# Own slots for the first gate, and an earlier place for the last tile's gates, in the recurrent branch of a two-layer streaming encoder

## The chip, the cores and the metric

The kernel runs on one core of one Trainium2 chip. The metric is the device time of one execution in microseconds (us), as the median of three runs. Profiles and traces come from one further execution that was taken with the hardware profiler; times inside it are counted from the start of its span.

Of the engines, PE is TensorE (matmuls into PSUM), ACT is ScalarE (activations, casts), DVE is VectorE, POOL is GpSimd, and SP issues nearly all DMAs. Each of them works through its own instructions in a fixed order and waits on semaphores of the others.

## What is computed

The reference is two layers over 1152 tokens (1024 of a prompt, 8 samples of 16). The change lies in layer 0, in the recurrent branch of its mixer, so only that is shown. `xr` and `gr` are two 512-wide column groups of one input projection.

```python
def causal_conv(xr, buf, w, b):
    t = xr.shape[1]
    xp = jnp.concatenate([buf.astype(xr.dtype), xr], axis=1)
    y = xp[:, 0:t] * w[0] + b
    for i in range(1, CONV_W):
        y = y + xp[:, i:i + t] * w[i]
    return y, xp[:, -(CONV_W - 1):]

def rg_lru(xc, h0, wa, ba, wx, bx, lam):
    ...
    r = jax.nn.sigmoid(jnp.einsum('btnc,ncd->btnd', xb, wa).reshape(bsz, t, D_LRU) + ba)
    gi = jax.nn.sigmoid(jnp.einsum('btnc,ncd->btnd', xb, wx).reshape(bsz, t, D_LRU) + bx)
    log_a = -LRU_C * r.astype(jnp.float32) * jax.nn.softplus(-lam.astype(jnp.float32))
    a = jnp.exp(log_a)
    bterm = jnp.sqrt(-jnp.expm1(2.0 * log_a)) * (gi * xc).astype(jnp.float32)
    bterm = bterm.at[:, 0].add(a[:, 0] * h0.astype(jnp.float32))
    ...
    _, h = lax.associative_scan(combine, (a, bterm), axis=1)

    # in even_mixer
    xc, new_buf = causal_conv(xr, conv_buf, conv_w, conv_b)
    hs, new_h = rg_lru(xc, h0, wa, ba, wx, bx, lam)
    rec = hs * jax.nn.gelu(gr)
    out = jnp.concatenate([att, rec], axis=-1) @ w_out
```

The rest of layer 0 is sliding-window attention, the output projection and an MLP; layer 1 is a gated MLP with a spatial mixing and a second MLP.

## The kernel before, in words

Everything is kept feature-major: 128 features lie on the partitions and the tokens run along the free dimension. The recurrent branch has 512 features, so four feature tiles, c = 0 to 3. The tokens are cut into three blocks of 384 (`NB`). A float32 matmul is done as three passes (`three`, L531 to L533) over a high and a low part of both operands; one bank of a projection is 8 slices of the contraction times 3 passes, so 24 matmuls.

For each feature tile there are three kinds of steps, and `LRU_ORDER` (L267) sets the order in which the program writes them:

- `x` with a number is one block of the first branch (`xr_bank`): 24 matmuls, and DVE scales the bank into `pad` (L679, L681). After the third block the convolution is queued in the background list: one ACT pass (L575), three DVE passes into `y` (L578), and the split of the result into `xch` (ACT, L586) and `xcl` (DVE, L590).
- `G` is `gates(c)`: two gates of three column pieces each, so six PSUM banks (`ax`) of 3 matmuls, 18 matmuls for a tile, each bank read by an ACT sigmoid (L613) into a tile `rg` of the gate. The first gate, `rg0`, is r and becomes a; the second, `rg1`, is gi and becomes the input of the recurrence. `gates` then queues in the background the rest of the recurrence: gi times y on POOL (L633), tanh, exp and sqrt on ACT (L624, L627, L630), two products on DVE (L636, L639), the samples' start states (L644 to L646), the scan on DVE (L649), which writes the state tile `h`, and two small copies of `h` on POOL (L653, L654).
- `g` is one block of the second branch (`gr_bank`): 24 matmuls, DVE scales the bank into `u` (L696), and after the third block ACT applies a gelu (L700) and POOL multiplies `h` by it (L703, L705).

`pump` hands out background work and splits of weights (`W.split`, L200 and L201: an ACT cast into the high part, a DVE subtraction into the low part) between the banks. The Tile framework then schedules all of it: each engine gets one fixed list of instructions that may differ from the written order. From the attention's first instruction on the recorded order is kept by the helper at L257.

The buffers matter here. `lr("rg", ...)` (the pool `lru`, two buffers to a tag) has two slots for all eight gate tiles: `rg0` and `rg1` of a tile take both, so the next tile's sigmoids can't write before this tile's scan has read them. The tag `xb` has four slots of 128 partitions and some 1176 floats: the four input tiles xin0 to xin3 at first, and later the four states `h`. The tag `y` has two slots for the convolution results. There are five `ax` banks, so PE can compute five of a tile's six gate banks ahead of the sigmoids. `raw` has two slots for loaded weights, and 12 split halves (`w`, `wx`) are alive at most in this stage, so the last two halves of the attention's q weights (w28 and w29) take slots that the last `g` bank frees.

After the last `g` block comes the attention. Its first token tile needs 24 matmuls for q and 24 for k and v (L257, `mm` from `w` and `xn0h`, `xn0l`, `xn1h`, `xn1l`; eight steps of three q and three kv matmuls), ACT copies both banks into `raw`, POOL squares it into `rstd`, DVE and POOL do the norm and the rotation, and PE transposes the result (`tp` from `xa`). PE does the second token tile's 48 matmuls before that first transpose.

Of the kernel before, what the change touches and what calls it, by code (L numbers as in the profile page):

```python
# [10 lines left out]
F32 = mybir.dt.float32  # L11
# [8 lines left out]
P = 128  # L20
# [12 lines left out]
CW = PADW - 3  # L33
# [230 lines left out]
         "n25 s06 s07 m11 f0 n27 m01 s10 n21 s11 s12 n23 s13 n20 s14 s15 s20 s16 n26 n22 F0 s21 n24 m02 e00 m12 s22 s23 "  # L264
         "s17 e10 s24 s25 f1 s26 s27 F1 e01 e11 f2 F2 e02 e12")

LRU_ORDER = [(t[0], int(t[1])) for t in "x2 x2 x2 x3 G0 g0 x3 G1 g0 x3 G2 g0 g1 g1 g1 g2 g2 g2 G3 g3 g3 g3".split()]  # L267

NKT, NVV, NPB = 3, 3, 3
QEV = False  # L270
# [11 lines left out]
def body(ctx, tc, io):  # L282
    nc = tc.nc

    def pool(name, bufs=1, space=None):
        kw = {} if space is None else {"space": space}
        return ctx.enter_context(tc.tile_pool(name=name, bufs=bufs, **kw))
# [4 lines left out]
    xp = pool("x")  # L292
# [31 lines left out]
    def bank(tag):  # L324
        bank.n += 1
        p = banks[tag if tag in ("mm", "two") else "ax"].pool
        return p.tile([P, 1024 if tag == "two" else 512], F32, tag=tag, bufs=BANKS[tag], name=f"{tag}{bank.n}")
# [47 lines left out]
    order += [(("xr", 0), [xr[0]], None), (("xr", 1), [xr[1]], None)]  # L375
    for kind, c in LRU_ORDER:
        key = {"x": ("xr", c), "G": ("gate", c // 2), "g": ("gr", c)}[kind]
# [21 lines left out]
    def pump(act, dve, pl, halves=1):  # L399
        W.pump(halves)  # L400
        bg.pump(act, dve, pl)
# [13 lines left out]
    def lr(tag, name, shape=None, dt=F32):  # L415
        return lrp.tile(shape or [P, CW], dt, tag=tag, bufs=2, name=name)
# [113 lines left out]
    def three(ps, wh, wl, ah, al, start, stop):  # L530
        nc.tensor.matmul(ps, wh, ah, start=start, stop=False)  # L531
        nc.tensor.matmul(ps, wh, al, start=False, stop=False)  # L532
        nc.tensor.matmul(ps, wl, ah, start=False, stop=stop)  # L533
# [38 lines left out]
    def add_conv(c):  # L572
        def c0():
            conv[c] = lr("y", f"y{c}")
            nc.scalar.activation(conv[c], pads[c][:, 0:CW], AF.Identity, bias=lc[:, c, 4:5], scale=lc[:, c, 0:1])  # L575

        def ci(i):
            nc.vector.scalar_tensor_tensor(conv[c], pads[c][:, i:i + CW], lc[:, c, i:i + 1], conv[c], OP.mult, OP.add)  # L578
            if i == 3:
                nc.gpsimd.tensor_scalar_mul(st[:, c, 0, 1:4], pads[c][:, SEQ:SEQ + 3], 1.0)  # L580
                nc.gpsimd.tensor_scalar_mul(st[:, c, 1:9, 1:4],
                                     pads[c][:, S0:].rearrange("p (b w) -> p b w", w=SW)[:, :, DS:SW], 1.0)

        def hi():
            conv[c, "h"] = lr("xc", f"xch{c}", dt=F32R)
            nc.scalar.copy(conv[c, "h"], conv[c])  # L586

        def lo():
            conv[c, "l"] = lr("xc", f"xcl{c}", dt=F32R)
            nc.vector.tensor_sub(conv[c, "l"], conv[c], conv[c, "h"].bitcast(F32))  # L590

        bg.add(("c0", c), (1200, 0, 0), c0)
        for i in (1, 2, 3):
            bg.add(("ci", c, i), (0, 1300, 0), lambda i=i: ci(i))
        bg.add(("xch", c), (1200, 0, 0), hi)
        bg.add(("xc", c), (0, 1300, 0), lo)

    def gates(c):
        bg.require(("xc", c))
        if c:  # L600
            bg.require(("rec", c - 1))
        wh, wl = W.get(("gate", c // 2))
        n = CW // 3
        out = []
        for g in range(2):
            t = lr("rg", f"rg{g}{c}")
            out.append(t)
            w = slice((c % 2 * 2 + g) * P, (c % 2 * 2 + g + 1) * P)
            for j in range(3):
                ps = bank("ax")  # L610
                cols = slice(j * n, j * n + n)
                three(ps[:, :n], wh[:, w], wl[:, w], conv[c, "h"][:, cols], conv[c, "l"][:, cols], True, True)
                nc.scalar.activation(t[:, cols], ps[:, :n], AF.Sigmoid, bias=lc[:, c, 5 + g:6 + g])  # L613
                pump(300, 800, 2000, 1 if j < 2 else 0)
        if c % 2:
            W.free(("gate", c // 2))
        if c < 3:
            add_conv(c + 1)
        r, gi = out
        th = G[c] = xp.tile([P, PADW], F32, tag="xb", bufs=4, name=f"h{c}")  # L620
        y = conv[c]

        def tanh():
            nc.scalar.activation(th[:, :CW], r, AF.Tanh, scale=spc[:, 0, c:c + 1])  # L624

        def exp():
            nc.scalar.activation(r, r, AF.Exp, scale=spc[:, 1, c:c + 1])  # L627

        def sqrt():
            nc.scalar.activation(th[:, :CW], th[:, :CW], AF.Sqrt)  # L630

        def bx():
            nc.gpsimd.tensor_mul(gi, gi, y)  # L633

        def beta():
            nc.vector.scalar_tensor_tensor(th[:, :CW], r, 1.0, th[:, :CW], OP.add, OP.mult)  # L636

        def bb():
            nc.vector.tensor_mul(gi, gi, th[:, :CW])  # L639

        def starts():
            a0, b0 = r[:, S0:CW:SW], gi[:, S0:CW:SW]
            h = small[:, 2, 0:DB]
            nc.vector.tensor_mul(h, a0, lc[:, c, 8:16])  # L644
            nc.vector.tensor_add(b0, b0, h)
            nc.vector.memset(a0, 0.0)  # L646

        def scan():
            nc.vector.tensor_tensor_scan(th[:, :CW], r, gi, 0.0, OP.mult, OP.add)  # L649

        def last():
            hs = th[:, S0:].rearrange("p (b w) -> p b w", w=SW)
            nc.gpsimd.tensor_scalar_mul(st[:, c, 0, 0:1], th[:, SEQ - 1:SEQ], 1.0)  # L653
            nc.gpsimd.tensor_scalar_mul(st[:, c, 1:9, 0:1], hs[:, :, DS - 1:DS], 1.0)  # L654

        bg.add(("bx", c), (0, 1300, 0), bx)
        bg.add(("tanh", c), (1200, 0, 0), tanh)
        bg.add(("exp", c), (1200, 0, 0), exp)
        bg.add(("sqrt", c), (2500, 0, 0), sqrt)
        bg.add(("beta", c), (0, 1300, 0), beta)  # L660
        bg.add(("bb", c), (0, 1300, 0), bb)
        bg.add(("starts", c), (0, 300, 0), starts)
        bg.add(("scan", c), (0, 1300, 0), scan)
        bg.add(("rec", c), (0, 0, 200), last)
# [48 lines left out]
    for step in START.split():  # L713
# [11 lines left out]
        elif kind == "m":  # L725
            c, nb = n
# [5 lines left out]
    seen = {}  # L732
    for kind, c in LRU_ORDER:
        if kind == "G":
            gates(c)
        else:
            nb = seen[kind, c] = seen.get((kind, c), -1) + 1
            (xr_bank if kind == "x" else gr_bank)(c, nb)
# [10 lines left out]
    def at(name, shape, dt=F32, tag=None, bufs=1):  # L749
        return ap_.tile(shape, dt, tag=tag or name, bufs=bufs, name=name)  # L750
# [23 lines left out]
    y = at("y", [P, 10])  # L774
# [1031 lines left out]
```

## Time and profile before

| | |
|---|---|
| time, median of 3 runs | 2216.12 us (2213.75 to 2217.06) |
| the profiled execution | 2215.67 us, of which its span 2213.9 us |
| mean granted TensorE clock | 0.992 |
| moved by DMA | 377.91 MB, mean 171 GB/s |

The recurrent branch runs from about 50 to 165 us of the span; the attention begins at 149 us. A row of the timeline gives start, duration, engine, line, operation, tiles (output<-inputs), shapes and count, and in brackets the engine's idle time just ahead of it with the instruction that ended it. A row of the groups gives line, engine, operation, tiles, shapes and count, then busy time and mean ns of one, then the idle time ahead of them. A row of the waits says who waited for whom: us in total, times, longest. The windows give for each stretch its length, then busy time and count for each engine and the granted clock of TensorE.

### The profile page before, as it was taken

The page shows a single profiled execution, that of the slowest core. Times are in us where ns is not written, and L with a number is a line of the kernel's source. Part 1 is how long each engine was busy: PE and PEld are TensorE (multiplying, and loading weights), DVE is VectorE, ACT ScalarE, POOL GpSimd, SP SyncE. Part 2 cuts the span into 40 slices and gives each one's busy share as a digit, 9 for nine tenths or more (in the row PEclk, how much of TensorE's full clock was granted, in tenths as well). Part 3 has the DMA queues.
Part 4 walks back from the last instruction along what each step waited for, and adds up shares of the span by engine and source line. Part 5 has one row for each costly group of instructions (what it writes and reads, how often), then busy time and mean ns, then how long its engine had stood idle before and what let it go on. Part 6 is the DMA issues. An engine that isn't in the chain of part 4 may idle for free.

```text
span 2213.9 us, 37892 instructions
## 1 busy us (share of the span) xinstructions
PE 2157.8 (97%) x14980; PEld 2114.9 (96%) x14980; DVE 1614.8 (73%) x2810; ACT 961.8 (43%) x1695; POOL 279.4 (13%) x332
## 2 busy tenths in 40 slices
PE   7989999899999999999999999989999999999999
PEld 7978989899999999999988899989999999999999
DVE  8778883798777678777793734269877777877776
ACT  5665663367666642112162123226766665211211
POOL 5147642000000000000050333100000000000000
PEclk9999999999999999999999999999999999999999
DMA  4110043237666777356751013322766667735574
GB/s 156 63 51 9 13 142 103 67 124 278 241 224 243 264 297 291 102 188 248 254 181 50 20 48 109 113 75 94 292 240 231 234 250 308 282 128 205 209 249 149
DMA packets 108003, 377.91 MB, mean 171 GB/s; under 512 B 13473, under 2 KB 24737, under 8 KB 107809
## 3 DMA queue, kind: packets, MB, share of 16 engines
q1 hardware_dynamic: 107680, 375.47, 47.1%
q8 instruction: 118, 1.93, 0.4%
q14 instruction: 61, 0.49, 0.1%
q10 hardware_dynamic: 144, 0.02, 0.0%
HBM read 240.09 MB, written 136.26 MB: 170 GB/s over the span
## 4 chain that ended last, share of the span: by engine, by line
PE 88%; DVE 6%; ACT 2%; issue 2%; DMA 1%; POOL 1%; SPq 0%; ACTq 0%; DVEq 0%; POOLq 0%
PE two L1293 64%; PE mm L533 5%; PE mm L531 5%; PE mm L532 5%; PE mm L257 2%; PE mm L1610 1%; PE mm L1612 1%; PE mm L1611 1%; DVE w L201 1%; PE pv L257 1%; PE tp L257 1%; PE ax L1639 1%; PE qk L257 1%; DVE b L407 0%; DVE x L1492 0%
## 5 line engine op out<-in xcount | busy, mean ns | idle before, releaser
L1293 PE MATMUL two<-b,w 128*128 128x288 f32 x5424 | 728.0, 296 | 12.4 <-DVE x L1137 12.4
L1293 PEld LDWEIGHTS two<-b,w 128*128 128x128 f32 x5424 | 726.7, 189 | 12.9 <-ACT tmp L478 12.9
L1293 PE MATMUL two<-h,w 128*128 128x288 f32 x4704 | 630.6, 295 | 3.2 <-DVE x L1492 1.5
L1293 PEld LDWEIGHTS two<-h,w 128*128 128x128 f32 x4704 | 627.5, 188 | 5.1 <-issue 3.0
L200 ACT CAST w<-raw 128x512 fp32r<-128x512 f32 x542 | 331.2, 620 | 645.9 <-PE two L1293 412.7
L201 DVE TENSOR_TENSOR w<-raw,w 128x512 fp32r<-128x512 f32 x542 | 386.4, 718 | 113.7 <-ACT w L200 111.5
L1492 DVE TENSOR_TENSOR x<-two,x 128x576 f32<-128x576 f32 x448 | 336.3, 754 | 127.9 <-PE two L1293 126.4
L531 PE MATMUL mm<-xn0h,w 128*128 128x384 f32 x372 | 127.8, 343 | 6.3 <-ACT xn0h L527 5.9
L532 PE MATMUL mm<-xn1l,w 128*128 128x384 f32 x372 | 125.6, 338 | 1.1 <-DVE xn1l L528 1.1
L533 PE MATMUL mm<-xn0h,w 128*128 128x384 f32 x372 | 126.3, 340 | 0.0
L532 PE MATMUL mm<-xn0l,w 128*128 128x384 f32 x372 | 126.3, 340 | 0.0
L531 PE MATMUL mm<-xn1h,w 128*128 128x384 f32 x372 | 125.9, 339 | 0.0
L533 PE MATMUL mm<-xn1h,w 128*128 128x384 f32 x372 | 125.7, 338 | 0.0
L1542 POOL TENSOR_TENSOR s<-s,tmp 128x384 f32<-128x384 f32 (+1 forms) x28 | 28.9, 1059 | 730.7 <-ACT tmp L1541 730.6
L1293 PE MATMUL two<-hk,w 128*128 128x288 f32 x672 | 91.2, 295 | 0.0
L407 DVE TENSOR_TENSOR ho<-c_a,ho 128x576 fp32r<-128x576 f32 x78 | 57.2, 753 | 46.1 <-ACT ho L406 46.0
L1293 PEld LDWEIGHTS two<-hk,w 128*128 128x128 f32 x672 | 90.1, 188 | 0.0
L1322 ACT ACTIVATE c_a<-c_a 128x1152 f32<-128x1152 f32 x60 | 70.1, 1168 | 19.3 <-DVE c_a L1404 18.0
L531 PEld LDWEIGHTS mm<-xn0h,w 128*128 128x128 f32 x372 | 71.0, 191 | 7.3 <-ACT xn0h L527 6.6
L407 DVE TENSOR_TENSOR ho<-c_b,ho 128x576 fp32r<-128x576 f32 x96 | 72.3, 753 | 2.5 <-ACT ho L406 2.5
L480 POOL TENSOR_TENSOR s<-s,tmp 128x384 f32<-128x384 f32 x49 | 54.7, 1121 | 148.2 <-ACT tmp L478 146.0
L1137 DVE TENSOR_TENSOR x<-mm,x 128x384 f32<-128x384 f32 x48 | 26.7, 555 | 63.8 <-PE mm L533 63.6
(287 smaller groups left out, 2815.3 us busy)
## 6 DMA issues: line engine op xcount, KB each, us to landing
hidden<-ho SPq DMA_DIRECT2D x196, 576.0 KB, 4.0
h<-hidden SPq DMA_DIRECT2D x196, 576.0 KB, 6.6
raw<-in_w SPq DMA_DIRECT2D x136, 512.0 KB, 4.5
x<-scratch SPq DMA_DIRECT2D x24, 576.0 KB, 7.7
scratch<-x SPq DMA_DIRECT2D x48, 192.0 KB, 1.8
raw<-in_wo SPq DMA_DIRECT2D x16, 512.0 KB, 3.6
xin<-in_xT SPq DMA_DIRECT2D x24, 192.0 KB, 4.2
x<-in_xT SPq DMA_DIRECT2D x8, 576.0 KB, 3.8
```

The costliest lines, as they stand in the source:

```text
L200: nc.scalar.copy(t[:, 0], src)
L201: nc.vector.tensor_sub(t[:, 1], src, t[:, 0].bitcast(F32))
L257: return lambda *a, **k: self.tc.keep_in_program_order(op(*a, **k))
L407: nc.vector.tensor_sub(lo, src, hi.bitcast(F32))
L480: (nc.vector if sum_on_dve else nc.gpsimd).tensor_add(ssum[nb], ssum[nb], sq)
L531: nc.tensor.matmul(ps, wh, ah, start=start, stop=False)
L532: nc.tensor.matmul(ps, wh, al, start=False, stop=False)
L533: nc.tensor.matmul(ps, wl, ah, start=False, stop=stop)
L1293: nc.tensor.matmul(o, w, a[:, c], start=first and k == 0 and i == 0, stop=k == len(pairs) - 1 and i == 2, skip_group_check=True)
L1322: nc.scalar.activation(o, o, AF.Relu) if fn == "relu" else nc.scalar.square(o, o)
L1492: nc.vector.tensor_add(o, both(ps), o)
L1542: nc.gpsimd.tensor_add(o, o, sq)
```

## The change

```diff
-LRU_ORDER = [(t[0], int(t[1])) for t in "x2 x2 x2 x3 G0 g0 x3 G1 g0 x3 G2 g0 g1 g1 g1 g2 g2 g2 G3 g3 g3 g3".split()]
+LRU_ORDER = [(t[0], int(t[1])) for t in "x2 x2 x2 x3 G0 g0 x3 g0 G1 x3 g0 g1 G2 g1 g1 G3 g2 g2 g2 g3 g3 g3".split()]
...
         for g in range(2):
-            t = lr("rg", f"rg{g}{c}")
+            if g:
+                t = lr("rg", f"rg{g}{c}")
+            elif c < 3:
+                t = xp.tile([P, CW], F32, tag="xb", bufs=4, name=f"rg{g}{c}")
+            else:
+                t = lr("y", f"rg{g}{c}")
```

The first gate of tiles 0, 1 and 2 moves into the slots of the tag `xb`, that of tile 3 into a slot of the tag `y`; the two slots of `rg` then hold second gates alone. No operation is added or taken away. In the order, G1 goes one block later, G2 two blocks later, and G3 moves from behind the three blocks of g2 to ahead of them. The lines behind the change have numbers that are five higher (L613 is now L618).

The lists of ACT show what becomes of this. In the names the digits ahead of the underscore tell the tile: `rg01` is gate 0 of feature tile 1, `xch3` the high part of tile 3's convolution, `u2` the second branch of tile 2, `w28` a half of the q weights, `ax25` a PSUM bank. First the place behind tile 0's sqrt, before:

```order
L630 ACTIVATE h0_754<-h0_754 128x1176
L200 CAST w11_517<-raw6_506 128x512 [waits DMAHW5_49]
L200 CAST w12_545<-raw7_515 128x512 [waits DMAHW6_49]
L200 CAST w13_548<-raw7_515 128x512
L200 CAST w14_559<-raw8_520 128x512 [waits DMAHW7_49]
L200 CAST w15_562<-raw8_520 128x512
L613 ACT_TABLE_LOAD [waits DVE_49,PE_49]
L613 ACTIVATE rg01_831<-ax25_832,lc_135 128x392 [waits Activation_49]
```

The same place of the changed kernel:

```order
L635 ACTIVATE h0_754<-h0_754 128x1176
L618 ACT_TABLE_LOAD
L618 ACTIVATE rg01_857<-ax26_858,lc_135 128x392 [waits PE_49]
L618 ACTIVATE rg01_857<-ax27_863,lc_135 128x392 [waits PE_49]
L200 CAST w11_517<-raw6_506 128x512 [waits DMAHW5_49]
L200 CAST w12_543<-raw6_506 128x512
L200 CAST w13_548<-raw7_515 128x512 [waits DMAHW6_49]
L618 ACTIVATE rg01_857<-ax28_868,lc_135 128x392 [waits PE_49]
```

The sigmoids of tile 1 now stand right behind tile 0's sqrt and wait for PE alone; the wait for DVE, which was tile 0's scan, is gone.

Second, ACT between the gates of tile 2 and those of tile 3, before (the split `xch3` and tile 2's tanh stand in the two rows ahead):

```order
L700 ACT_TABLE_LOAD
L700 ACTIVATE u1_1057<-u1_1057 128x1152 [waits DVE_49]
L627 ACT_TABLE_LOAD
L627 ACTIVATE rg02_943<-rg02_943,spc_151 128x1176 [waits Activation_49]
L630 ACT_TABLE_LOAD
L630 ACTIVATE h2_983<-h2_983 128x1176
L700 ACT_TABLE_LOAD
L700 ACTIVATE u2_1151<-u2_1151 128x1152 [waits DVE_49]
L200 CAST w24_1271<-raw13_1045 128x512 [waits DMAHW4_49]
L200 CAST w25_1304<-raw13_1045 128x512
L613 ACT_TABLE_LOAD [waits DVE_49,PE_49]
L613 ACTIVATE rg03_1208<-ax46_1209,lc_135 128x392 [waits Activation_49]
```

And now:

```order
L575 ACTIVATE y3_1073<-pad3_718,lc_135 128x1176 [waits Pool_49]
L629 ACTIVATE h2_1047<-rg02_1015,spc_151 128x1176 [waits DVE_49,Activation_49]
L705 ACT_TABLE_LOAD
L705 ACTIVATE u1_1004<-u1_1004 128x1152 [waits DVE_49]
L632 ACT_TABLE_LOAD
L632 ACTIVATE rg02_1015<-rg02_1015,spc_151 128x1176 [waits Activation_49]
L586 CAST xch3_1106<-y3_1073 128x1176 [waits DVE_49]
L635 ACT_TABLE_LOAD
L635 ACTIVATE h2_1047<-h2_1047 128x1176
L618 ACT_TABLE_LOAD [waits PE_49]
L618 ACTIVATE rg03_1126<-ax43_1127,lc_135 128x392 [waits Pool_49]
```

Tile 2's tanh now waits for DVE: its output `h2` takes a slot of `xb` that tile 1's first gate leaves when tile 1's scan has read it. The split `xch3`, which tile 3's gate matmuls need, stands behind that tanh, a gelu and an exp. Tile 3's sigmoids no longer wait for a scan, and stand ahead of u2's gelu.

Third, the end of the stage on ACT, before:

```order
L627 ACT_TABLE_LOAD
L627 ACTIVATE rg03_1208<-rg03_1208,spc_151 128x1176 [waits Activation_49]
L630 ACT_TABLE_LOAD
L630 ACTIVATE h3_1240<-h3_1240 128x1176
L200 CAST w27_1344<-raw14_1269 128x512
L700 ACT_TABLE_LOAD [waits DVE_49]
L700 ACTIVATE u3_1277<-u3_1277 128x1152 [waits Pool_49]
L200 CAST w28_1432<-raw15_1307 128x512 [waits DMAHW6_49,PE_49]
L200 CAST w29_1435<-raw15_1307 128x512 [waits PE_49]
L257 ACTIVATE raw_1375<-mm55_1394,rT_149 128x512 [waits DVE_49,PE_49,Activation_49]
```

And now:

```order
L635 ACTIVATE h3_1166<-h3_1166 128x1176
L200 CAST w26_1291<-raw14_1135 128x512 [waits DMAHW5_49,PE_49]
L200 CAST w27_1294<-raw14_1135 128x512 [waits PE_49]
L200 CAST w28_1432<-raw15_1195 128x512 [waits DMAHW6_49,PE_49]
L200 CAST w29_1435<-raw15_1195 128x512 [waits PE_49]
L705 ACT_TABLE_LOAD
L705 ACTIVATE u3_1299<-u3_1299 128x1152 [waits DVE_49]
L257 ACTIVATE raw_1375<-mm55_1394,rT_149 128x512 [waits DVE_49,PE_49]
```

The casts of the last q weights, w28 and w29, now stand ahead of u3's gelu instead of behind it. From the attention's first matmul on, each engine's list is the same as before. On SP the loads of gr1 and of the second gate weights change places; on POOL the last memset of the attention's buffers goes ahead of the product of `h3` and `u3`.

## The prediction

> **What bounds the kernel now.** I read the page first (its head and the chain that ended last), then the windows of the recurrent branch, then the waits and the timeline there.
>
> ```profile
> span 2213.9 us, 37892 instructions
> ...
> PE 88%; DVE 6%; ACT 2%; issue 2%; DMA 1%; POOL 1%; SPq 0%; ACTq 0%; DVEq 0%; POOLq 0%
> ```
>
> PE is the bound and carries 88% of the chain. The change takes no matmul away, so all it can win is PE time lost to waits, and only before the attention, since from there on the lists are unchanged. So I ask what PE loses between the first matmul that changes place and the first transpose of the attention.
>
> ```profile
> 79.28 0.33 PE L531 MATMUL ax<-xch,w 128*128 128x392 f32 x1
> 122.46 0.44 PE L531 MATMUL ax<-xch,w 128*128 128x392 f32 x1 [3.41 <-ACT rg L613]
> 148.98 0.63 PE L257 MATMUL mm<-w,xn0h 128*128 128x512 f32 x2
> 158.00 0.79 PE L257 MATMUL mm<-w,xn1h 128*128 128x512 f32 x1 [2.58 <-ACT w L200]
> 161.26 0.79 PE L257 MATMUL mm<-w,xn1h 128*128 128x512 f32 x1 [2.47 <-DVE w L201]
> 164.71 0.63 PE L257 MATMUL mm<-w,xn0h 128*128 128x512 f32 x2
> 173.10 0.63 PE L257 MATMUL mm<-w,xn0h 128*128 128x512 f32 x2
> 175.79 0.54 PE L257 MATMUL tp<-identr,xa 128*128 128x128 f32 x4 [1.83 <-DVE xa L257]
> ```
>
> From the waits of 75 to 176 us (us in total, times, longest):
>
> ```profile
> ACT L613 <- DVE h L649: 13.5, 3, 7.4
> ...
> PE ax L531 <- ACT rg L613: 5.2, 3, 3.4
> ...
> PE ax L532 <- DVE xcl L590: 1.8, 2, 1.5
> ```
>
> Stretch one is 79.28 to 148.98 us, the rest of the branch. Stretch two is 148.98 (first q matmul) to 175.79 (first transpose). In stretch one PE waited 5.2 us for sigmoids to empty a bank and 1.8 us for `xcl`. The first row is the cause: the sigmoids of the next tile waited 13.5 us in three pieces for the scan, whose gate tiles they overwrite. In stretch two PE waited for the casts of the last q weights.
>
> **Stretch one, part by part.** Work left there: 12 banks of 24 matmuls and three tiles with 18 gate matmuls each, 342 in all.
>
> ```profile
> core 0: us, PE busy (x) PEld busy (x) DVE busy (x) ACT busy (x) POOL busy (x), PEclk, DMA share, GB/s
> 96.10:122.46 26.36, 21.50 (x120) 20.86 (x120) 19.38 (x19) 18.85 (x24) 9.73 (x5) 1.00 0.25 81
> 122.46:127.00 4.54, 4.54 (x17) 4.52 (x18) 3.30 (x4) 4.54 (x7) 2.14 (x2) 0.62 0.00 0
> 127.00:149.00 22.00, 21.03 (x121) 20.71 (x120) 11.82 (x14) 17.09 (x21) 8.67 (x8) 1.00 0.07 25
> ```
>
> At the undisturbed pace of the last row, 21.03/121 = 0.174 us, the 342 take 59.5 us. They took 69.70, so 10.2 us were lost: 7.0 in waits, 1.6 in the window behind the long wait, where the clock was 0.62 (17 matmuls in 4.54 us instead of 2.96), and 1.6 that I can't place. Own slots remove the sigmoids' wait for the scan; what is late next I find by walking the new ACT and DVE lists with these durations:
>
> ```profile
> 84.01 1.19 ACT L630 ACTIVATE h<-h 128x1176 f32<-128x1176 f32 x1
> ...
> L200 ACT CAST w<-raw 128x512 fp32r<-128x512 f32 x16 | 9.4, 621 | 4.9 <-DMA raw<-in_gr 4.9
> L613 ACT ACTIVATE rg<-ax,lc 128x392 f32<-128x392 f32 x18 | 9.0, 596 | 0.0
> L624 ACT ACTIVATE h<-rg,spc 128x1176 f32<-128x1176 f32 x3 | 4.0, 1317 | 0.0
> L627 ACT ACT_TABLE_LOAD x3 | 3.8, 1283 | 0.1
> L627 ACT ACTIVATE rg<-rg,spc 128x1176 f32<-128x1176 f32 x3 | 3.8, 1280 | 0.0
> L700 ACT ACTIVATE u<-u 128x1152 f32<-128x1152 f32 x3 | 3.5, 1171 | 0.0
> L586 ACT CAST xch<-y 128x1176 fp32r<-128x1176 f32 x2 | 2.4, 1209 | 0.0
> L578 DVE SCALAR_TENSOR_TENSOR y<-pad,lc,y 128x1176 f32<-128x1176 f32 x6 | 10.7, 1788 | 0.0
> L649 DVE TENSOR_TENSOR_SCAN h<-rg,rg 128x1176 f32<-128x1176 f32 x3 | 7.8, 2598 | 0.0
> L590 DVE TENSOR_TENSOR xcl<-y,xch 128x1176 fp32r<-128x1176 f32 x3 | 7.3, 2427 | 2.8 <-ACT xch L586 2.8
> ```
>
> Up to tile 0's sqrt nothing moves (tile 0's own first gate only changes its slot: its sigmoids still wait for PE alone in the list); the sqrt ends at 85.2. *Tile 1*: load 1.28, so the first sigmoid ends near 87.1. PE reaches the sixth bank of that tile after 24 + 15 + 8 matmuls, at 87.5: no wait. *Tile 2*: PE reaches its gates 16 + 3 + 48 matmuls later, at 99.2, and `xcl` is due near 95, behind tile 0's scan and three splits. Its sixth bank comes at 107.4; ACT gets to the first sigmoid there at 107.0, behind casts, a gelu and tile 1's sqrt. *Tile 3*: PE is there at 118.9. ACT ends tile 2's six sigmoids at 110.5, then a convolution pass, the tanh (which waits until tile 1's scan ends, near 112.0), load and gelu, load and exp: `xch` can start at 118.4 and ends at 119.6, if DVE's three convolution passes (3 x 1.79 from 112.5) end at 117.9. So PE waits about 0.8 us, and up to 0.7 more for `xcl`. I take 1.5 us, bounded by 0 and 3, because those passes meet a POOL product. Such meetings are dear:
>
> ```profile
> 112.22 3.51 POOL L703 TENSOR_TENSOR h<-h,u 128x1024 f32<-128x1024 f32 x1 [9.93 <-issue]
> 113.41 3.57 DVE L578 SCALAR_TENSOR_TENSOR y<-pad,lc,y 128x1176 f32<-128x1176 f32 x1
> ```
>
> The pass took 3.57 us beside a product, twice its mean. The convolution of tile 3 is the one thing that now has little cover. Of the unplaced 1.6 us I keep half. Stretch one then saves 10.2 - 1.5 - 0.8 = 7.9 us, bounded by 10.2 - 3 - 1.6 = 5.6 and 10.2. Swapping the loads of gr1 and the second gate weights costs nothing in this walk: both land before their casts. If a cast has to wait for its load all the same, one wait is at most the 4.9 us of the row above; it would hold up the sigmoids queued behind it.
>
> The ACT list has as many table loads as before. The Trainium skill, page "ScalarE: Activation LUTs", section "What ACT_TABLE_LOAD costs", puts a switch at about 2.66 us, a load of 1.283 and a drain of 1.38. By the page, the two loads ahead of tile 3's `xch` would make it 2.8 us later, and the forecast below would be some 2203.4. The trace has the 1283 ns, but 0.1 us of idle time ahead of three loads and none behind them, so I go by the row.
>
> **Stretch two.** It took 26.81 us. PE's own work in it is 16 steps of 1.049 us ((173.10 - 164.71)/8) and three matmuls, some 17.4. The other engines' rows there, from their own timelines:
>
> ```profile
> 164.49 1.05 ACT L257 ACTIVATE raw<-mm,rT 128x512 f32<-128x512 f32 x2 [6.02 <-PE mm L257]
> 158.02 2.61 DVE L649 TENSOR_TENSOR_SCAN h<-rg,rg 128x1176 f32<-128x1176 f32 x1
> 160.54 1.27 DVE L201 TENSOR_TENSOR w<-raw,w 128x512 fp32r<-128x512 f32 x2
> 162.35 2.38 POOL L703 TENSOR_TENSOR h<-h,u 128x1024 f32<-128x1024 f32 x1
> 164.69 0.56 POOL L705 TENSOR_TENSOR h<-h,u 128x128 f32<-128x128 f32 x1
> 165.68 0.84 POOL L257 TENSOR_TENSOR tab<-tab_raw,gain 128x256 f32<-128x256 f32 x1
> 166.48 1.25 POOL L257 TENSOR_TENSOR rstd<-raw 128x640 f32<-128x640 f32 x1
> ```
>
> The q weights' low parts were subtracted only behind tile 3's scan, which ended at 160.6. Now that recurrence starts three blocks earlier and the casts stand ahead of u3's gelu: cast and subtraction are due about 6 us after the last `g` matmul, PE wants them after six steps, 6.3 us. So that wait shrinks to 1 us at most. What is late next is POOL's square, 9.31 us ahead of the transpose in the old trace. By its data it can start 8 x 1.049 + 1.05 = 9.5 us into the stretch. By its queue: tile 3's scan ends about 5 us in (behind exp, sqrt and two products), then two state copies and two memsets (about 2.3), product and its small part (2.9), `tab` (0.8): 11.0. I take the middle, 10.3, so the transpose comes at 19.6 and the stretch saves 7.2 us, bounded by 8.0 and 6.5.
>
> **The sum.** 7.9 + 7.2 = 15.1 us off the profiled execution's 2215.67 (span 2213.9), which is 0.45 us under the median of the runs shown: 2200.6, bounded by 2197.5 (18.2 off) and 2203.6 (12.1 off). Behind the transpose every list is as before and nothing is tied to an absolute time, so the rest should shift as a block.
>
> **The rivals.** *Only stretch one gains.* POOL and DVE still hold up the attention: if tile 3's scan ends 7 us later than in my walk, the second stretch is as long as ever. That is 2215.7 - 7.9 = 2207.8. For it speaks that POOL, not PE, sets that start in my own sum; against it, that three blocks of PE work (12.5 us) now lie between tile 3's gates and the end.
>
> *A new wait at tile 3's gates.* Tile 2's tanh now waits for tile 1's scan, and `xch` of tile 3 is queued behind it. If one more convolution pass meets a product, and PE waits some 4.5 us instead of 1.5, the slow window comes back too: 3 + 1.6 less, 2205.2. For it speaks the 3.57 us pass; against it, that PE arrives only 0.8 us too early. The Trainium skill, page "TensorE: Matmul & The Clock Gate", Part 1, says that PE's clock halves after about 3.4 us of idleness; the trace agrees, 0.62 behind the 3.41 us wait.
>
> *Slower.* The same mechanism carried further: everything behind that tanh on ACT's list waits in order, the sigmoids of tile 3, two gelus and the q casts too. Each us of delay of `xch` costs PE one. To end 0.2% above the old time the delay must be 15.1 + 4.4 - 1.6 = 17.9 us beyond my walk, 2220.1. Three load waits of 4.9 us on the casts ahead of it come to 14.7, so even these would not do alone.
>
> *Nothing gained.* The wait moves but the sum stays, if DVE or ACT, not PE, paced the branch and the attention's start: 2215.7. Against it: in the window of 96.10 to 122.46 us both were busy for less than 19.4 of 26.36 us.
>
> **How the numbers follow.** Chances: forecast (2197.5 to 2203.6) 0.62, a new wait 0.16, only stretch one 0.13, nothing gained 0.05, slower 0.04. The likeliest gives 2200.6. The range goes from the forecast's lower bound to just over the rival where only stretch one gains, 2197.5 to 2208; that leaves out the last two cases and a fringe of the others. About 0.2% (4.4 us) is what a measurement of this kernel can tell from no change: faster 0.91, same 0.05, slower 0.04.
>
> **What would show it.** Right: no wait of a sigmoid's table load for the scan; PE's waits for `rg` and `xcl` together under 3 us; no window with a clock under 0.9 between 96 and 150 us; the first q matmul near 141 us and the first transpose near 160.7. Wrong: a tanh (L629) with long idle time ahead of it, PE waiting for `xch` at tile 3, q casts (L200) still ending a PE wait, or a transpose that has moved while the end has not.

## The result, and the profile after

| | before | changed |
|---|---|---|
| median of 4 runs each, same chip | 2215.03 us (2213.75 to 2217.06) | 2202.17 us (2200.97 to 2203.56) |
| ratio to before, 95% interval | | 0.9943 [0.9931, 0.9956] |
| the profiled execution, its span | 2215.67, 2213.9 us | 2200.97, 2199.2 us |

The change saves 12.9 us (0.6%). The forecast was 15.1 us, 2200.6; the time lies in the forecast's own bounds.

The page of the changed kernel, head and chain that ended last:

```profile
span 2199.2 us, 37893 instructions
...
PE 87%; DVE 7%; ACT 2%; issue 2%; DMA 1%; POOL 1%; SPq 0%; ACTq 0%; DVEq 0%; POOLq 0%
```

PE still carries the chain. Where the time came from, the windows of PE over the prediction's two stretches and the rest tell (length, then PE's busy time and matmul groups, then the granted clock). Before:

```profile
core 0: us, PE busy (x), PEclk, DMA share, GB/s
79.28:148.98 69.70, 62.64 (x344) 0.98 0.17 53
148.98:175.79 26.81, 19.93 (x101) 0.87 0.25 74
175.79:2213.90 2038.11, 2009.59 (x14197) 1.00 0.49 178
```

Changed:

```profile
77.88:141.44 63.56, 60.32 (x343) 1.00 0.23 69
141.44:161.41 19.97, 17.65 (x100) 1.00 0.23 67
161.41:2199.20 2037.79, 2010.02 (x14197) 1.00 0.49 178
```

Stretch one is 6.1 us shorter, stretch two 6.8, together 13.0; the rest shifted as a block. Length minus busy time is PE's idle time: 7.06 + 6.88 = 13.9 us before, 3.24 + 2.32 = 5.6 now, so 8.4 us of the gain are waits. The other 4.6 us are busy time: the same matmuls took 82.57 us before and take 77.97 now. Most of that is the clock, 0.98 and 0.87 in the two stretches before and 1.00 in both now: no slow window follows a wait in this execution. The spans also differ by 1.4 us ahead of stretch one (79.28 against 77.88). The lists there are alike, and in the runs below that start lies anywhere from 76.9 to 80.2 us; it is no effect of the change, and the medians, 12.9 us apart, agree with the 13.0.

The waits of PE from 75 to 165 us in the changed kernel, and the timeline's rows at the ends of the two large ones:

```profile
PE ax L531 <- ACT xch L586: 2.9, 1, 2.9
PE tp L257 <- DVE xa L257: 2.3, 1, 2.3
PE ax L531 <- ACT rg L618: 0.4, 1, 0.4
```

```profile
121.14 1.17 PE L531 MATMUL ax<-xch,w 128*128 128x392 f32 x5 [2.85 <-ACT xch L586]
141.44 0.63 PE L257 MATMUL mm<-w,xn0h 128*128 128x512 f32 x2
161.41 0.53 PE L257 MATMUL tp<-identr,xa 128*128 128x128 f32 x4 [2.32 <-DVE xa L257]
```

Of the old waits (5.2 us for sigmoids, 1.8 for `xcl`, 5.0 for the q casts) 0.4 us is left. Two remain that the prediction named: the split `xch` of tile 3, and the norm ahead of the first transpose. For the first, the timelines of ACT, DVE and POOL ahead of 121.14:

```profile
116.31 1.28 ACT L632 ACTIVATE rg<-rg,spc 128x1176 f32<-128x1176 f32 x1
119.92 1.17 ACT L586 CAST xch<-y 128x1176 fp32r<-128x1176 f32 x1 [2.32 <-DVE y L578]
111.51 3.40 DVE L578 SCALAR_TENSOR_TENSOR y<-pad,lc,y 128x1176 f32<-128x1176 f32 x1
114.95 1.45 DVE L578 SCALAR_TENSOR_TENSOR y<-pad,lc,y 128x1176 f32<-128x1176 f32 x1
116.43 3.46 DVE L578 SCALAR_TENSOR_TENSOR y<-pad,lc,y 128x1176 f32<-128x1176 f32 x1
109.76 3.91 POOL L638 TENSOR_TENSOR rg<-rg,y 128x1176 f32<-128x1176 f32 x1 [7.33 <-ACT rg L618]
115.17 3.47 POOL L708 TENSOR_TENSOR h<-h,u 128x1024 f32<-128x1024 f32 x1
```

ACT was ready for `xch` when its exp ended at 117.6, and stood 2.32 us for `y`. The three convolution passes of tile 3 took 8.37 us in all: 3.40 and 3.46 the two that began while a POOL product ran, and 1.45 the one between them, which began 0.22 us ahead of POOL's second product. For the second wait, the rows of stretch two:

```profile
143.65 2.60 DVE L654 TENSOR_TENSOR_SCAN h<-rg,rg 128x1176 f32<-128x1176 f32 x1
148.43 2.50 POOL L708 TENSOR_TENSOR h<-h,u 128x1024 f32<-128x1024 f32 x1
150.90 0.56 POOL L710 TENSOR_TENSOR h<-h,u 128x128 f32<-128x128 f32 x1
151.41 0.74 POOL L257 TENSOR_TENSOR tab<-tab_raw,gain 128x256 f32<-128x256 f32 x1
152.11 1.26 POOL L257 TENSOR_TENSOR rstd<-raw 128x640 f32<-128x640 f32 x1
```

POOL goes without a pause from the branch's last product to the square, which starts 10.67 us into the stretch; the transpose follows 9.30 us later.

### The profile page after: what moved, and what is told of

Its sections match the earlier page's. It is cut to its first block, busy times and chain, and to the rows that moved or that the text cites. A ratio compares the mean times of both kernels' runs of the same rounds, so it can differ in the third digit from the quotient of the medians.

```text
span 2199.2 us, 37893 instructions
## 1 busy us (share of the span) xinstructions
PE 2151.9 (98%) x14980; PEld 2110.6 (96%) x14980; DVE 1614.3 (73%) x2810; ACT 962.8 (44%) x1695; POOL 281.3 (13%) x332
## 4 chain that ended last, share of the span: by engine, by line
PE 87%; DVE 7%; ACT 2%; issue 2%; DMA 1%; POOL 1%; SPq 0%; ACTq 0%; DVEq 0%; POOLq 0%
PE two L1298 64%; PE mm L533 4%; PE mm L531 4%; PE mm L532 4%; PE mm L257 2%; PE mm L1615 1%; PE mm L1617 1%; PE mm L1616 1%; DVE w L201 1%; PE pv L257 1%; PE tp L257 1%; PE ax L1644 1%; PE qk L257 1%; DVE y L578 1%; DVE b L407 0%
## 5 line engine op out<-in xcount | busy, mean ns | idle before, releaser
L1298 PEld LDWEIGHTS two<-b,w 128*128 128x128 f32 x5424 | 727.2, 189 | 13.0 <-ACT tmp L478 12.9
L1327 ACT ACTIVATE c_a<-c_a 128x1152 f32<-128x1152 f32 x60 | 70.1, 1168 | 19.0 <-DVE c_a L1409 17.9
```

The costliest lines, as they stand in the source:

```text
L1298: nc.tensor.matmul(o, w, a[:, c], start=first and k == 0 and i == 0, stop=k == len(pairs) - 1 and i == 2, skip_group_check=True)
L1327: nc.scalar.activation(o, o, AF.Relu) if fn == "relu" else nc.scalar.square(o, o)
```

## The experiments

The theory is the prediction's: own slots let ACT run ahead of the scan, the new order turns that into an earlier start of the attention, and what is left are two waits that POOL's products cause. Its rivals: one of the two parts does it all, or what is saved ahead of the attention is given back. Each version was timed five times, e2 eleven times. In the table, one and two are the stretches in each profiled execution (they begin at the first matmul behind the bank x3.1, which is the second block of tile 3's first branch, and at the first q matmul, and end at the first transpose), idle and busy are PE's over both, rest is from the transpose to the end.

| run | median us (range) | one | two | idle | busy | rest |
|---|---|---|---|---|---|---|
| before, profiled | 2215.03 (2213.75 to 2217.06) | 69.70 | 26.81 | 13.9 | 82.6 | 2038.1 |
| changed, profiled | 2202.17 (2200.97 to 2203.56) | 63.56 | 19.97 | 5.6 | 78.0 | 2037.8 |
| e1, slots alone | 2205.06 (2203.83 to 2206.90) | 64.45 | 22.02 | 6.5 | 80.0 | 2039.4 |
| e2, order alone | 2212.76 (2209.18 to 2214.04) | 65.01 | 28.49 | 12.8 | 80.8 | 2041.0 |
| e3, G3 late again | 2204.93 (2202.68 to 2205.28) | 62.37 | 21.26 | 5.6 | 78.1 | 2041.1 |
| e4, one product on DVE | 2201.50 (2200.90 to 2203.53) | 62.08 | 19.48 | 3.5 | 78.1 | 2040.0 |
| e5, slots, G3 alone early | 2206.52 (2205.49 to 2207.37) | 66.77 | 21.13 | 8.0 | 79.9 | 2038.0 |
| e6, two products on DVE | 2205.43 (2201.17 to 2205.98) | 64.87 | 18.69 | 4.2 | 79.4 | 2041.4 |
| e7, all three on DVE | 2199.49 (2197.81 to 2201.37) | 62.05 | 18.68 | 2.7 | 78.1 | 2039.9 |
| e8, changed again | 2202.88 (2202.48 to 2203.59) | 64.91 | 19.30 | 4.8 | 79.4 | 2039.7 |
| e9, e7 again | 2198.07 (2197.09 to 2199.30) | 61.82 | 18.70 | 2.4 | 78.1 | 2038.2 |

e1 to e4, e5 to e7, and e8 with e9 shared a chip and its runs of the kernel before, which came to 2214.67, 2214.29 and 2214.08 us. Each ratio below is to those; a difference between medians of two such groups holds the difference between the chips as well.

### The slots alone

```diff
-LRU_ORDER = [(t[0], int(t[1])) for t in "x2 x2 x2 x3 G0 g0 x3 g0 G1 x3 g0 g1 G2 g1 g1 G3 g2 g2 g2 g3 g3 g3".split()]
+LRU_ORDER = [(t[0], int(t[1])) for t in "x2 x2 x2 x3 G0 g0 x3 G1 g0 x3 G2 g0 g1 g1 g1 g2 g2 g2 G3 g3 g3 g3".split()]
```

(Against the changed kernel; the new slots stay.)

> The new slots for the first gates, with the old order of the recurrent branch. Stretch one is from the end of bank x3.1 to the first q matmul (before 69.7 us, changed 63.6), stretch two from there to the attention's first transpose (before 26.8, changed 20.0). My theory: the slots end the sigmoids' waits for the scan, so stretch one comes to 61 to 65 us, but tile 3's gates are still last and the q casts still stand behind u3's gelu, so stretch two stays at 24 to 27; total 4 to 7 us under before. Rival, the order does the work: stretch one within 1.5 us of 69.7, total within 2 us of before.

Ratio 0.9955 [0.9943, 0.9968]: 9.6 us under the kernel before, where 4 to 7 were expected. Stretch one came as expected, stretch two was too long in the expectation. PE's waits of this run from 75 to 166 us:

```profile
PE tp L257 <- DVE xa L257: 3.6, 1, 3.6
PE ax L532 <- DVE xcl L590: 2.6, 2, 2.2
PE mm L257 <- DVE w L201: 0.2, 1, 0.2
```

The wait for the q weights is down to 0.2 us with G3 where it always stood. So the late casts of before were not a matter of where G3 stands in the program, nor of u3's gelu, behind which they still stand here (gelu at 144.71, casts at 145.79, against 156.28 and 157.35 before): ACT's list had been held up by the scans, and once it is not, the casts are in time. The slots alone carry three quarters of the gain or more (9.6 of 12.9 us, or of the 11.2 of e8 below).

### The order alone

```diff
-LRU_ORDER = [(t[0], int(t[1])) for t in "x2 x2 x2 x3 G0 g0 x3 G1 g0 x3 G2 g0 g1 g1 g1 g2 g2 g2 G3 g3 g3 g3".split()]
+LRU_ORDER = [(t[0], int(t[1])) for t in "x2 x2 x2 x3 G0 g0 x3 g0 G1 x3 g0 g1 G2 g1 g1 G3 g2 g2 g2 g3 g3 g3".split()]
```

(Against the kernel before; the old slots stay.)

> The new order, with the old two slots for all gates. My theory: the sigmoids still wait for the scans (10 us or more in all on ACT), so stretch one stays at 67 to 73 us; in stretch two tile 3's recurrence, itself held up by the scan of tile 2, still ends late: 22 to 27 us; total between 5 under before and 2 above it. Rival, the order carries the gain and the slots little: stretch one under 66, total 9 us or more under before.

Ratio 0.9986 [0.9977, 0.9994], 1.9 us under the kernel before. Both stretches missed their expected windows, one too long in the expectation, the other too short; that the sum held is luck, since the two errors offset each other. First the waits of ACT, then those of PE, from 75 to 172 us:

```profile
ACT L613 <- DVE h L649: 14.6, 3, 5.9
```

```profile
PE mm L257 <- ACT w L200: 4.1, 1, 4.1
PE mm L257 <- DVE w L201: 2.6, 1, 2.6
PE ax L532 <- DVE xcl L590: 2.5, 2, 1.2
PE tp L257 <- DVE xa L257: 2.0, 1, 2.0
PE ax L531 <- ACT rg L613: 1.6, 2, 0.9
```

The sigmoids' table loads wait for the scan as long as before (14.6 us, 13.5 before); the later places of G1 and G2 only take PE out of their way. With the old slots the delay lands on the q casts, 6.7 us instead of 5.0. Alone, slots and order save 9.6 and 1.9 us, together 12.9 (11.2 in e8): nearly additive.

### Which move of the order counts

G3 put back behind the blocks of g2, the rest of the change kept:

```diff
-LRU_ORDER = [(t[0], int(t[1])) for t in "x2 x2 x2 x3 G0 g0 x3 g0 G1 x3 g0 g1 G2 g1 g1 G3 g2 g2 g2 g3 g3 g3".split()]
+LRU_ORDER = [(t[0], int(t[1])) for t in "x2 x2 x2 x3 G0 g0 x3 g0 G1 x3 g0 g1 G2 g1 g1 g2 g2 g2 G3 g3 g3 g3".split()]
```

> The changed kernel with G3 put back behind the three g2 blocks, all else as changed. On ACT the q casts still stand ahead of u3's gelu. My theory: the convolution of tile 3 gets cover, so the 2.9 us wait of PE for xch goes and stretch one falls to 60 to 62.5; but tile 3's scan ends later against the end of the branch and the low parts of the q weights and POOL's products stand behind it, so stretch two grows to 23 to 27; total 1 to 4 us above the changed kernel. Rival, the place of the casts ahead of the gelu is what shortened stretch two: it stays under 21.5 and the total is at or under the changed kernel's.

Ratio 0.9951 [0.9937, 0.9965], 2.8 us above the changed kernel in the median, timed on another chip, with ranges that touch and intervals that overlap: not told apart. Stretch one was as expected (PE no longer waits for `xch`), stretch two shorter than expected and within the rival's 21.5. Its first transpose waits 3.61 us, and a window of 5 us behind it has half the clock:

```profile
162.22 0.75 PE L257 MATMUL tp<-identr,xa 128*128 128x128 f32 x4 [3.61 <-DVE xa L257]
```

```profile
162.22:167.22 5.00, 5.00 (x23) 0.50 0.00 0
167.22:172.22 5.00, 5.00 (x32) 0.96 0.00 0
```

So with G3 late PE's idle time is the same 5.6 us, only in another place: less in stretch one, more in stretch two. What this execution lost on the changed one, 3.3 us, lies in the rest; some 2.5 of it is the half clock of those 5 us.

The reverse, with the slots kept, the old places of G1 and G2, and G3 alone moved ahead of g2 (against the changed kernel):

```diff
-LRU_ORDER = [(t[0], int(t[1])) for t in "x2 x2 x2 x3 G0 g0 x3 g0 G1 x3 g0 g1 G2 g1 g1 G3 g2 g2 g2 g3 g3 g3".split()]
+LRU_ORDER = [(t[0], int(t[1])) for t in "x2 x2 x2 x3 G0 g0 x3 G1 g0 x3 G2 g0 g1 g1 g1 G3 g2 g2 g2 g3 g3 g3".split()]
```

> The slots of the changed kernel with the old order, but G3 moved ahead of the three banks g2.0 to g2.2; G1 and G2 stay at their old places. Theory 1 (behind the slots, what the order adds is G3's place alone: with G3 early, tile 3's scan ends earlier, and the attention's first transpose no longer stands idle 3.6 us, which in the two runs that had such a wait was followed by a clock of 0.50 and 0.66): tile 3's scan starts 1 to 3 us into the second stretch (with the slots and the old order it started 4.7 us in, with the whole change 2.2), the second stretch lasts 20 to 21 us (22.0 and 20.0), the first 63 to 65 with a wait of PE for xch of tile 3, and the time is 1.5 to 3 us under that of the slots alone, within 1 us of the whole change. Theory 2 (G1 and G2 carry what the order adds, by tiles 1 and 2 finishing earlier): the scan stays near 4.7 us in, the second stretch near 22, and the time within 0.8 us of the slots alone.

Ratio 0.9959 [0.9947, 0.9972], 1.5 us above e1 in the median: neither theory. PE's waits from 75 to 165 us:

```profile
PE ax L532 <- DVE xcl L590: 2.6, 2, 2.2
PE ax L531 <- ACT xch L586: 2.2, 1, 2.2
PE mm L257 <- DVE u L701: 2.2, 1, 2.2
```

The first row is e1's: tile 1's gates, one block too early for `xcl`. The second is the price of an early G3, and the third a new one at the first q matmuls. The scan was even earlier than theory 1 wanted (1.5 us ahead of the first q matmul), but POOL's square did not follow it: it started 11.8 us into the stretch, behind ACT's raw copy. On top of the slots, moving G3 alone is worth nothing that these runs show. With G1 and G2 moved and G3 late (e3) the two stretches together last 83.6 us, as short as the whole change's 83.5, against 86.5 in e1 and 87.9 here. So in the stretches the moves of G1 and G2 bring what the order adds, and G3's only moves a wait from the transpose to tile 3's gates. In the times this can't be told apart: e1 and e3 are 9.6 and 9.7 us under the kernel before, the whole change 12.9 or 11.2.

### The two waits that are left

Tile 2's product gi times y on DVE instead of POOL, where it met tile 3's convolution (against the changed kernel):

```diff
-            nc.gpsimd.tensor_mul(gi, gi, y)
+            (nc.vector if c == 2 else nc.gpsimd).tensor_mul(gi, gi, y)
```

> The changed kernel with the product gi times y of tile 2 on DVE instead of POOL. In the changed kernel the three convolution passes of tile 3 take 8.37 us, beside a POOL product of 3.91 and one of 3.47. My theory, that meetings with POOL make the passes slow: with one meeting less they take 4.3 to 6.5 us; DVE has 1.4 us more ahead of them, so xch starts 0.5 to 2 us earlier and PE's wait for it falls from 2.9 to 0.5 to 2.3; total 0.5 to 2.5 us under the changed kernel. Rival, the passes are slow by themselves there or the exp ahead of xch on ACT sets it: passes over 7.5 us or a PE wait that stays at 2.9 or grows by the 1.4 us.

The convolution passes of tile 3 (least, median and greatest ns), in the changed kernel and here:

```profile
L578 DVE SCALAR_TENSOR_TENSOR y<-pad,lc,y x3: 1445/3400/3455, 111.5 to 116.4; 128x1176 f32<-128x1176 f32 x3
```

```profile
L578 DVE SCALAR_TENSOR_TENSOR y<-pad,lc,y x3: 1433/1434/1436, 114.9 to 118.7; 128x1176 f32<-128x1176 f32 x3
```

Here no product of POOL lies beside the passes, each takes 1.43 us, and PE's wait for `xch` falls from 2.85 to 0.40 us (0.7 is added for `xcl`). The edit did more than take one meeting away: ACT now runs u1's gelu behind the exp (at 119.47, exp at 116.88), so POOL's other product, which needs that gelu, starts at 120.78, behind the passes. Both meetings are gone, and that shows the cause of the slow passes. What is left of the wait is ACT's: `xch` now follows the gelu without a pause.

Ratio 0.9940 [0.9928, 0.9953]: only 0.7 us under the changed kernel in the median, less than can be told apart. The profiled execution, the slowest of the five at 2203.53 us, had a slow window behind its first transpose, and its rest is 2.2 us longer than the changed kernel's; whether the other four had one is not shown.

```profile
161.79:166.79 5.00, 5.00 (x27) 0.66 0.00 0
```

Tile 3's products h times u on DVE, so that POOL comes to the square sooner:

```diff
-        nc.gpsimd.tensor_mul(h, h, u[:, :SEQ])
+        e = nc.vector if c == 3 else nc.gpsimd
+        e.tensor_mul(h, h, u[:, :SEQ])
...
-        nc.gpsimd.tensor_mul(hs, hs, u[:, SEQ:].rearrange("p (b w) -> p b w", w=DS))
+        e.tensor_mul(hs, hs, u[:, SEQ:].rearrange("p (b w) -> p b w", w=DS))
```

> The changed kernel with the two products h times u of tile 3 (2.50 and 0.56 us on POOL, ahead of POOL's square of the first q rows) on DVE instead. Theory 1 (in the changed kernel POOL's two products of tile 3 set when the square starts, 10.7 us into the second stretch): the square starts 1 to 2 us earlier, right behind ACT's raw copy, the transpose 0.8 to 1.5 us earlier, the second stretch lasts 18.5 to 19.2 us against 20.0, and the time is 0.8 to 1.5 us under the changed kernel. Theory 2 (the square waits for something else as well, or DVE's list, longer by some 1.5 us, hands it on later): the second stretch stays at 19.7 or above, the time is the same or up to 1.5 us above.

```profile
152.96 1.25 POOL L257 TENSOR_TENSOR rstd<-raw 128x640 f32<-128x640 f32 x1 [2.18 <-ACT raw L257]
```

The square now waits for ACT's raw copy and starts 9.37 us into the stretch, 1.3 earlier, and stretch two falls to 18.69: theory 1. The time did not follow, 2205.43 us, ratio 0.9948 [0.9934, 0.9961], and the profile says where it went: stretch one, whose instructions the edit leaves alone, took 64.87 instead of 63.56 us, at nearly the same wait for `xch`, 3.0 us, with a clock of 0.87 and 0.85 behind it, and the rest 3.6 us more. On the time neither theory was right.

```profile
118.00:124.00 6.00, 2.98 (x14) 0.87 0.00 0
124.00:130.00 6.00, 6.00 (x31) 0.85 0.14 22
```

Both edits together:

> The changed kernel with both: tile 2's product gi times y and tile 3's products h times u on DVE. If both waits are what the trace shows (2.85 us of PE for xch of tile 3, of which 2.4 went with the first edit alone, and POOL's products ahead of the square), the first stretch lasts 61.8 to 62.5 us, the second 18.2 to 19, and the time is 2 to 3 us under the changed kernel, with the clock behind the first transpose at 0.9 or above. If what is saved ahead of the transposes is given back behind them, as the first edit alone showed (first stretch 1.5 shorter, second 0.5 shorter, time 0.7 under), the stretches are as short, a clock of 0.5 to 0.7 stands in the 5 us behind the first transpose, and the time is within 1 us of the changed kernel.

Ratio 0.9929 [0.9917, 0.9942], 2199.49 us. Both stretches are as short as expected, and no slow window followed the transpose.

### Changed kernel and best version side by side

> The changed kernel itself, timed beside the version with tile 2's product gi times y and tile 3's products h times u on DVE, on one chip, since the two were timed on different occasions so far (2202.17 and 2199.49 us). If the waits that these products cause are worth what the traces show (1.5 us of the first stretch, 1.3 of the second), the changed kernel stands 2 to 3.5 us above that version. If the difference between the two was the chip's, they stand within 1 us of each other. The trace shows which clock dips the changed kernel has this time: by the traces so far the part behind the first transpose takes 2037.8 to 2041.4 us, the longer the more the clock dips in it; if the dips go by the execution and not by the kernel, this execution may show another length than its 2037.8 with the same waits in the two stretches (2.85 for xch, 2.3 ahead of the transpose).

> The version with tile 2's product gi times y and tile 3's products h times u on DVE, beside the changed kernel. First theory (the two waits are worth their length): first stretch near 62, second near 18.7, the time 2 to 3.5 us under the changed kernel. Second theory (what is saved there is lost elsewhere): within 1 us of it.

2202.88 us, ratio 0.9948 [0.9935, 0.9960], against 2198.07, 0.9926 [0.9913, 0.9940]: 4.8 us apart, with ranges that do not touch. That is more than the 2 to 3.5 expected. The two profiled executions are 5.3 us apart: 2.4 are PE's idle time in the two stretches, as expected, 1.3 are busy time there, and some 1.5 lie in the rest. The busy time is the clock; the windows around the wait for `xch`, first in the changed kernel's profile shown above, then in this second one:

```profile
118.00:124.00 6.00, 3.15 (x18) 1.00 0.00 0
124.00:130.00 6.00, 6.00 (x35) 1.00 0.28 85
```

```profile
118.00:124.00 6.00, 3.17 (x12) 0.79 0.00 0
124.00:130.00 6.00, 6.00 (x33) 0.93 0.26 74
```

One program, one wait (2.85 and 2.83 us), two clocks. In the second execution the matmuls behind it started 0.32 instead of 0.18 us apart for some 3.7 us, and stretch one was 64.91 us long, 1.35 more. Half of that came back: the first transpose then waited 1.66 us and not the 2.3 expected, and stretch two was 0.67 shorter. The version with DVE's products has no wait above 1.1 us left in either profile:

```profile
PE tp L257 <- DVE xa L257: 1.1, 1, 1.1
PE ax L532 <- DVE xcl L590: 0.7, 1, 0.7
PE ax L531 <- ACT xch L586: 0.4, 1, 0.4
PE ax L531 <- ACT rg L618: 0.3, 1, 0.3
```

So it wins the waits, and in these two profiles no slow window stands in the stretches or behind the transpose. It beats both kernels.

## Why the prediction was right, and where a size was off

**PE bounds, and only waits can be won.** Right in the main: the rest took 2037.8 us against 2038.1. But waits are 8.4 of the 13.0 us; the other 4.6 are matmul time, of which stretch one's part, 2.3, is close to the 2.4 in the sum (10.2 - 7.0 - 0.8).

**Own slots take the sigmoids' wait for the scan away.** Right, and e1 and e2 show that it is the slots that do it. At tile 1 no wait was forecast and none came; at tile 2 0.39 us came, where ACT was forecast 0.4 us ahead.

**Stretch one, 7.9 us: mis-sized, 6.1 came.** The term is PE's wait at tile 3's gates. I took 1.5 us, with bounds of 0 and 3; it came to 2.85 for `xch`, and 3.24 us with the 0.39 at tile 2. The walk counts in times of the profile before, where stretch one starts at 79.28; now it starts at 77.88, so 1.4 us come off each of its times. It was then right within 0.8 us on ACT (exp due to end at 117.0, it did at 117.6) and on PE's arrival (117.5; 118.3). It failed at "three convolution passes (3 x 1.79 from 112.5) end at 117.9", which is 111.1 and 116.5 here: they began at 111.5 and ended at 119.9, 3.4 us late. The 1.79 was a mean over six passes of which one had met a POOL product, 3.57 + 5 x 1.43 = 10.7; here two of three began beside one, at 3.40 and 3.46. I had the 3.57 us pass before me and spread it over all. With none met, e4 has the wait at 0.40. PE waiting for `xch` at tile 3 stood in my list of what would show the prediction wrong; it came, and it is this term. The other part of the term, half of the unplaced 1.6 us kept, was right: busy time in stretch one is 60.32 us, 0.8 over the 59.5 for full pace.

**Stretch two, 7.2 us: 6.8 came.** The square was forecast 10.3 us into the stretch and started at 10.67; queue, not data, set it, which e6 confirms: without the products in its queue it starts at 9.37, by the data's 9.5. The middle that I took, 10.3, had no ground: the later of the two dates sets the start, and by the queue alone I had 11.0, which would have made the saving 6.5. That 7.2 and 6.8 lie so close is in part luck. The reason that I gave for the earlier casts, tile 3's recurrence three blocks earlier, was only part of it: e1 has the casts in time without that move.

**The rival that only stretch one gains** needed tile 3's scan to end 7 us later than in my walk, about 5 us into the stretch; it ended 4.8 us in. Not even the slots alone leave stretch two as it was (22.0 us). **The new wait at tile 3's gates** came in kind, at 2.85 us, short of the 4.5; the slow window that it expected stood behind that wait in e8, not in the first profile. **Slower** and **nothing gained** found nothing for them: `xch` started 2.9 us later than in my walk (117.0, with the 1.4 us off; 119.9), not 17.9, and the casts' waits for loads were 1.1 us in all.

**The table loads.** The exp above starts at 116.31, and its load ran from 115.02 to 116.30: no drain shows, as the row said, and the Trainium skill's 2.66 us for a switch ("ScalarE: Activation LUTs", "What ACT_TABLE_LOAD costs") does not hold in this profile.

**No window under 0.9.** True in the first profile, and not a property of the kernel: e8 has 0.79 behind the same wait.

## What to carry to other kernels

A tile that two stages share through a small pool is a dependency on the engine that reads it last; if a list of instructions waits on it in order, the waits appear later and at other engines, so give it its own slot before moving any program order. When DVE and POOL work side by side, price each pass by what lies beside it, not by its mean. And count a wait of PE of some two us or more as able to cost more than its length. By the windows here the slow clock added nothing behind some, an estimated 1.7 us behind others (5 us at 0.66) and 2.5 at most (5 us at 0.50). So clearing several such waits together may pay where clearing one shows nothing; that is argued from a few executions.

## What the runs showed of the hardware

**A clock that falls behind some waits and not behind others, and after shorter ones than I thought.** Waits of 1.84 (e4), 2.83 (e8), 3.02 (e6) and 3.61 us (e3) were followed by windows with a clock of 0.66, 0.79, 0.87 and 0.50; waits of 2.85 and 2.32 us in the changed kernel's first profile, 1.99 in e2 and 1.83 in the kernel before by 1.00. In e5 two waits of 2.17 us each, for `xch` and at the first q matmuls, were followed by 0.66 and by 1.00. So length alone does not decide; what does was not tried. The Trainium skill, page "TensorE: Matmul & The Clock Gate", Part 1, has the clock halve after an idle window of about 3.4 us, and says that the window runs freely, not from the start of the wait. That waits of one length end both ways agrees with a free window; that 1.84 us suffices does not agree with one that must be idle throughout.

**The clock elsewhere moves the total as well.** The rest has the same instructions in all runs and took 2037.8 to 2041.4 us. It goes with dips of the clock; the 50 us from 950 us behind the transpose in e5 (rest 2038.0, clock 1.00) and e6 (2041.4, clock 0.93) are one place of several. What sets off these dips was not tried.

```profile
1116.31:1166.31 50.00, 46.23 (x289) 1.00 0.57 183
```

```profile
1112.28:1162.28 50.00, 46.20 (x277) 0.93 0.56 184
```

**A DVE pass and a POOL product exclude each other.** The first slow pass ended at 114.91, 1.24 us behind the end of POOL's product at 113.67; the other at 119.89, 1.25 behind 118.64. In e6 both distances are 1.24. Alone a pass takes 1.43. So it did its work almost wholly behind the product, not at half speed beside it. The pass in the middle shows the reverse: it began ahead of POOL's second product and took 1.45, while that product took 3.47, against the 2.50 of its like at 148.43. The Trainium skill, page "SBUF — State Buffer", section "Who interferes with whom", says that for a DVE instruction with two inputs in SBUF: it shares a read port with a GpSimd instruction that reads SBUF, and the later of the two is held until the other has finished. These rows agree.
